# The lead-in of a transformer layer: small loads on another queue, the first conditioning columns computed another way

## The chip, the cores and the metric

The kernel runs on one core of a Trainium2 chip. Five engines take part, each with an instruction queue of its own that is worked off in order: TensorE (PE; its weight loads are listed as PEld), VectorE (DVE), ScalarE (ACT), GpSimd (POOL) and SyncE (SP), which here issues the DMA transfers. SBUF is the on-chip memory of 128 partitions; PSUM holds the sums of TensorE in banks of 128 x 512 FP32 numbers. The metric is the time of one execution in microseconds.

## The reference

One layer of a diffusion transformer in FP32: 256 latent tokens and 256 context tokens of width 2048. Cut to what matters here:

```
m = silu(cond) @ w_ada + b_ada             # cond: c for latent, c_ctx for context; w_ada: 2048 x 12288
sh1, sc1, g1, sh2, sc2, g2 = split(m, 6)
h = (x * (1 + sc1) + sh1) @ w_in           # latent;  w_in: 2048 x 3072
h_ctx = (ctx * (1 + csc1) + csh1) @ w_in   # context, with its own columns of m
... two kinds of attention over h and h_ctx, w_out, layer norm, SwiGLU FFN, layer norm
```

Before the first product with `w_in` can start, the conditioning vectors c and c_ctx must have gone through silu and through the columns of `w_ada` that belong to the first 128 features (a shift and a scale for each of the two token kinds), the first 128 columns of x and ctx must have been transposed and modulated, and the first rows of `w_in` must be there.

## The kernel before

Every large product is made of three products in a rounded FP32 form: a factor is split into a high part (a cast by ScalarE) and a low part (the remainder, by DVE), and TensorE adds high x high, high x low and low x high (`mm3`, L271 to L273). One such trio for a 128-token row block and 512 output columns takes three 128x512 products.

The first stage, the input projection, goes over the 16 blocks of 128 features in five groups of 1, 1, 2, 4 and 8 blocks (`GROUPS`). For group g the kernel needs:

- its conditioning columns (`flow_columns`): for shift and for scale the 2048 rows of `w_ada`, 128 columns per block. The weights are the moving operand, the columns of silu(c) the stationary one (`cs`, 32 columns wide); four partial sums land in four strips of a PSUM bank (L546). ScalarE copies them to SBUF (L571), TensorE adds the strips through a selection matrix (L576), and DVE adds the bias columns (L582, L584). The bias columns come from `brow`, a load of `b_ada` that TensorE transposes (L334).
- its part of x and ctx (`flow_part`, L608 and L613), transposed on TensorE (L633), modulated by ScalarE from PSUM into `uf` (L639), cast to the high part `uh` (L646), and subtracted by DVE to the low part `ul` (L649).
- its rows of `w_in` (`flow_weights`, loads at L473, high parts L495, low parts L498), in six blocks of 512 columns. Blocks 2 and 5 are keys and values and have four row blocks (two latent, two context); the others are queries and have two.

`flow_products` issues the trios, and `evac` (L696 to L700) takes the sums out of PSUM.

The order of all this is not the order in which it is written. `Flow` is a planner: each step is added with its engine, an assumed length, the steps that it follows and the buffers that it takes and gives back. `run` lays the steps out in time, engine by engine: whenever an engine is free, the ready step of lowest rank whose buffers are free goes next. Ranks are then recomputed from the latest start of each step, and the best of eight rounds is emitted. On the chip each engine works in that order, with real waits. The planner begins each engine at a given time (`F`'s second argument). Weights are loaded into six buffers of 1 MB (`raw`, four, and `araw`, two); 18 buffers of 512 KB (`b4`) hold modulated inputs, keys, values and other things.

56 warm-up steps (`warm_step`, L1130; two records each) are products of the identity that nobody reads. They depend on nothing but each other and have the lowest rank, so that the planner puts one wherever it sees TensorE free and no other step ready. They hold one of four PSUM work banks from the first to the last of them.

Ahead of the flow, in program order, stand the loads of c, c_ctx and `b_ada` (L311 to L314), the transpose of c and c_ctx (L316), its silu on ScalarE (L319) and the transpose of `b_ada`.

Of the kernel before, what the change touches and what calls it, by code (L numbers as in the profile page):

```python
# [196 lines left out]
def dit_layer(ctx: ExitStack, tc: tile.TileContext, x, c, cx, c_ctx, w_ada, b_ada, w_in, q_norm_g,  # L197
# [112 lines left out]
    crow = pa.tile([2 * KD, P], F32, tag="crow", name="crow")  # L310
    nc.sync.dma_start(crow[0:KD, :], c.rearrange("o (k p) -> (o k) p", p=P))  # L311
# [156 lines left out]
    def flow_load(w, k0, nk, c0, width, where=("raw", "araw")):  # L468
        room = Buf(*where)

        def fn():
            room.t = pools[room.pool].tile([P, G4 * NB], F32, tag="raw", name="raw")[:, : nk * width]
            nc.sync.dma_start(  # L473
                room.t.rearrange("p (k n) -> p k n", k=nk),
                w[k0 * P : (k0 + nk) * P, c0 : c0 + width].rearrange("(k p) n -> p k n", p=P),
            )

        return room, F.add("SP", dma_ns(nk * width * P * 4, width * 4), fn, take=[room])

    def flow_weights(w, k0, nk, c0, width=NB, where=("raw", "araw"), spare=False):  # L480

        raw, ld = flow_load(w, k0, nk, c0, width, where)
        pieces = []
        for s in range(0, nk * width, SUB * NB):
# [28 lines left out]

    def flow_products(hl, deps, ready, cols, ps, xs, first, last, prev):
# [16 lines left out]
    last_load = []  # L531

    def flow_columns(c0, ncol, shift, scale, ats, at):
# [18 lines left out]
        for g in range(ns):  # L552
# [3 lines left out]
            ns1 = nk / 4 * (40 + 1.67 * width)  # L556
            if c0:
                def both(g=g, r0=r0, r1=r1):
                    fn(g, 0, r0, 0, nk)
                    fn(g, 1, r1, 0, nk)  # L560

                prev = F.add("PE", 2 * ns1 + 420, both, [l0, l1, prev], [bank] if g == 0 else [], [r0, r1])
            else:
                prev = F.add("PE", ns1, lambda g=g, r=r0: fn(g, 0, r, 0, nk), [l0, prev], [bank] if g == 0 else [], [r0])
                prev = F.add("PE", ns1, lambda g=g, r=r1: fn(g, 1, r, 0, nk), [l1, prev], [], [r1])
        F.at = at
# [11 lines left out]
        def add(i):  # L578
# [4 lines left out]
            else:  # L583
                nc.vector.scalar_tensor_tensor(scale, pv[:, :, 1, :], 1.0, bc, op0=ALU.add, op1=ALU.add)  # L584

        a = F.add("ACT", 60 + 0.9 * width, copy, [prev], [sb], [bank])
        b = F.add("PE", 224 * ncol, sums, [a], [ps], [sb])
        return a, [F.add("DVE", 160, lambda i=i: add(i), [b], give=[ps]) for i in range(2)]

    u = {}  # L590

    def flow_inputs(g, span):
# [8 lines left out]
    def flow_part(k0, n, at, each):  # L601
# [13 lines left out]

        F.at = at + 0.5 * each if k0 else -2.0
        ns = dma_ns(n * P * SEQ * 4, n * P * 4)
        loads = [F.add("SP", max(ns, 500), load_x), F.add("SP", max(ns, 500), load_cx, take=[cx_room])]
        for s in range(2):
# [3 lines left out]
            for j0 in range(0, n, 2):  # L623
# [24 lines left out]
                def rest(rooms=rooms, j0=j0, nj=nj, uf=uf):  # L648
                    nc.vector.tensor_tensor(rooms[1].t[:, j0 : j0 + nj, :], uf.t[:, :nj, :],  # L649
                                            rooms[0].t[:, j0 : j0 + nj, :].bitcast(F32), op=ALU.subtract)  # L650

                p = F.add("PE", 205 * nj, flip, [loads[s], copy if k0 else None], [ps], [cx_room] if s else [],
                          at=None if k0 else -1.0)
                for j in range(nj):
# [7 lines left out]
    def flow_block(g, b, chunks):  # L662
# [10 lines left out]
        for (hl, deps), cols in chunks:  # L673
            kk = k0 + done
            base = kk - (kk - k0) % G4
            for r in rows:
# [3 lines left out]
                def operand(j, rooms=rooms, r=r):  # L680
# [463 lines left out]

    flow_inputs(0, (0.0, 0.0))
    T = 18.0
# [478 lines left out]
```

## Time and profile before

| | us |
|---|---|
| median of 3 runs | 1141.15 |
| lowest and highest run | 1140.55, 1144.86 |
| profiled execution: its span, which is its own time here | 1139.7 |
| first weight load issued by SyncE | 3.09 |
| first product with `w_in` | 18.58 |

The page of the profile has busy times per engine, the span in slices, the DMA queues, the chain of work that ended last, the costliest groups of instructions and the DMA issues. The views used below are: busy time by stretches (for each engine the busy microseconds and, in brackets, the number of instructions; then the granted clock of TensorE, the mean busy share of the 16 DMA engines and the GB/s that they moved); the timeline of an engine (start, duration, engine, line, operation, output<-inputs, shapes, count; in brackets the idle time before it and what ended it); groups of instructions by line (count, busy time, mean ns, idle time before them); waits (who waited for whom, in total, how often, the longest); and the chain of waits (start, duration, what). A busy TensorE is not necessarily doing needed work: the warm-up products count as busy.

### The profile page before, as it was taken

How to read it: one execution, taken by the hardware profiler on the slowest of the kernel's cores; microseconds unless marked ns; L12 is line 12 of the kernel's file. 1: busy time of each engine (PE TensorE's matmuls, PEld its weight loads, DVE VectorE, ACT ScalarE, POOL GpSimd, SP SyncE). 2: the span in 40 equal slices, each digit the busy share in tenths (PEclk: the TensorE clock that was granted, in tenths of full speed). 3: DMA queues.
4: the chain of work that ended last, by engine and by line, in shares of the span. 5: the costliest groups of instructions: out<-in, count | busy, mean ns of one | idle time of the engine just before them, and what ended most of it. 6: DMA issues, size and time to landing. Idle time of an engine off the chain costs nothing.

```text
span 1139.7 us, 14229 instructions
## 1 busy us (share of the span) xinstructions
PE 1119.6 (98%) x5347; PEld 905.9 (79%) x5347; DVE 828.2 (73%) x1053; ACT 546.7 (48%) x784; POOL 42.2 (4%) x82
## 2 busy tenths in 40 slices
PE   8999999999999999999999999999999999999995
PEld 8766678788887787888888888888888888888884
DVE  4753589899989896867767566776766787676556
ACT  3332454877874365444464444445444344333441
POOL 1000040110100000010000000000000000000000
PEclk9999999999999999999999999999999999999998
DMA  8999999776999688988866776677677888877531
GB/s 257 392 381 384 396 379 356 259 250 200 369 350 386 230 325 323 317 314 307 310 203 237 235 240 222 219 256 258 205 263 241 311 314 332 319 270 266 190 135 74
DMA packets 178078, 321.28 MB, mean 282 GB/s; under 512 B 8620, under 2 KB 42828, under 8 KB 175703
## 3 DMA queue, kind: packets, MB, share of 16 engines
q1 hardware_dynamic: 178008, 320.36, 80.2%
q8 instruction: 42, 0.69, 0.2%
q14 instruction: 28, 0.23, 0.1%
HBM read 304.07 MB, written 16.25 MB: 281 GB/s over the span
## 4 chain that ended last, share of the span: by engine, by line
PE 90%; DMA 5%; DVE 3%; ACT 1%; issue 0%; POOL 0%; SPq 0%; DVEq 0%; POOLq 0%; ACTq 0%
PE acc L271 27%; PE acc L273 27%; PE acc L272 27%; DMA raw<-in_w_ada_dram 2%; PE wk L546 2%; PE wk L939 2%; PE wk L1130 1%; DMA raw<-in_w_in_dram 1%; DMA raw<-in_w_out_dram 1%; DMA pd<-hx 1%; PE wk L271 1%; PE wk L273 1%; PE wk L272 1%; PE wk L633 1%; PE wk L992 0%; DVE lo L498 0%
## 5 line engine op out<-in xcount | busy, mean ns | idle before, releaser
L262 DVE TENSOR_TENSOR lo<-raw,hi 128x1024 fp32r<-128x1024 f32 x258 | 312.0, 1221 | 181.8 <-ACT hi L261 178.5
L261 ACT CAST hi<-raw 128x1024 fp32r<-128x1024 f32 x258 | 270.7, 1055 | 334.3 <-PE acc L273 296.3
L272 PE MATMUL acc<-lo,u2h 128*128 128x512 f32 x704 | 274.0, 389 | 0.8 <-DVE lo L262 0.8
L271 PE MATMUL acc<-hi,u2h 128*128 128x512 f32 x704 | 274.7, 390 | 0.0
L273 PE MATMUL acc<-hi,u2l 128*128 128x512 f32 x704 | 274.1, 389 | 0.1
L271 PEld LDWEIGHTS acc<-hi,u2h 128*128 128x128 f32 x704 | 132.2, 188 | 28.3 <-ACT u2h L1448 0.8
L272 PEld LDWEIGHTS acc<-lo,u2h 128*128 128x128 f32 x704 | 132.2, 188 | 28.2 <-DVE lo L262 1.1
L273 PEld LDWEIGHTS acc<-hi,u2l 128*128 128x128 f32 x704 | 132.2, 188 | 28.1 <-DVE u2l L1449 0.6
L495 ACT CAST hi<-raw 128x1024 fp32r<-128x1024 f32 (+1 forms) x86 | 87.8, 1031 | 116.8 <-DMA raw<-in_w_in_dram 63.8
L271 PE MATMUL acc<-hi,hTh 128*128 128x512 f32 x344 | 135.5, 394 | 0.0
L273 PE MATMUL acc<-hi,hTl 128*128 128x512 f32 x344 | 133.9, 389 | 0.0
L272 PE MATMUL acc<-lo,hTh 128*128 128x512 f32 x344 | 133.9, 389 | 0.0
L381 DVE SCALAR_TENSOR_TENSOR adav<-raw,cs,adav 128x512 f32<-128x512 f32 (+1 forms) x128 | 121.3, 948 | 13.4 <-DMA raw<-in_w_ada_dram 11.2
L498 DVE TENSOR_TENSOR lo<-raw,hi 128x1024 fp32r<-128x1024 f32 (+1 forms) x86 | 101.6, 1194 | 29.1 <-ACT hi L495 28.8
L271 PE MATMUL acc<-hi,uh 128*128 128x512 f32 x256 | 102.5, 400 | 0.2 <-ACT hi L495 0.2
L272 PE MATMUL acc<-lo,uh 128*128 128x512 f32 x256 | 100.2, 391 | 1.7 <-DVE lo L498 1.5
L273 PE MATMUL acc<-hi,ul 128*128 128x512 f32 x256 | 100.0, 390 | 0.0
L272 PEld LDWEIGHTS acc<-lo,hTh 128*128 128x128 f32 x344 | 64.6, 188 | 14.4 <-issue 1.0
L271 PEld LDWEIGHTS acc<-hi,hTh 128*128 128x128 f32 x344 | 64.6, 188 | 14.2 <-issue 0.7
L273 PEld LDWEIGHTS acc<-hi,hTl 128*128 128x128 f32 x344 | 64.6, 188 | 13.3
L271 PEld LDWEIGHTS acc<-hi,uh 128*128 128x128 f32 x256 | 48.1, 188 | 16.5 <-issue 5.9
L272 PEld LDWEIGHTS acc<-lo,uh 128*128 128x128 f32 x256 | 48.1, 188 | 11.8 <-DVE lo L498 2.6
(205 smaller groups left out, 1149.2 us busy)
## 6 DMA issues: line engine op xcount, KB each, us to landing
raw<-in_w_ada_dram SPq DMA_DIRECT2D x72, 1024.0 KB, 7.7
raw<-in_w_gate_dram SPq DMA_DIRECT2D x44, 1024.0 KB, 5.2
raw<-in_w_up_dram SPq DMA_DIRECT2D x44, 1024.0 KB, 5.3
raw<-in_w_down_dram SPq DMA_DIRECT2D x44, 1024.0 KB, 4.9
raw<-in_w_ada_dram SPq DMA_DIRECT2D x48, 512.0 KB, 5.5
raw<-in_w_in_dram SPq DMA_DIRECT2D x18, 1024.0 KB, 7.4
raw<-in_w_out_dram SPq DMA_DIRECT2D x16, 1024.0 KB, 8.0
pd<-hx SPq DMA_DIRECT2D x64, 128.0 KB, 3.8
```

The lines of the kernel that those rows point to most:

```text
L261: nc.scalar.copy(hi[:, :n], raw[:, s : s + n])
L262: nc.vector.tensor_tensor(lo[:, :n], raw[:, s : s + n], hi[:, :n].bitcast(F32), op=ALU.subtract)
L271: nc.tensor.matmul(ps, lhsT=xh, rhs=w[0], start=first, stop=False, skip_group_check=seeded)
L272: nc.tensor.matmul(ps, lhsT=xh, rhs=w[1], start=False, stop=False, skip_group_check=seeded)
L273: nc.tensor.matmul(ps, lhsT=xl, rhs=w[0], start=False, stop=last, skip_group_check=seeded)
L381: nc.vector.scalar_tensor_tensor(a[:, c : c + piece], raw[:, f : f + piece], cs[:, 4 * (g * (G4 * NB // w) + j) + 2, None], a[:, c : c + p ...
L495: nc.scalar.copy(hl.hi[:, :n], raw.t[:, s : s + n])
L498: nc.vector.tensor_tensor(hl.lo[:, :n], raw.t[:, s : s + n], hl.hi[:, :n].bitcast(F32), op=ALU.subtract)
L546: nc.tensor.matmul(bank.t[32 * j : 32 * j + 32, :width], lhsT=cs[:, 4 * k + 2 - 2 * i : 4 * k + 34 - 2 * i], rhs=raw.t[:, c * width : (c + ...
L633: nc.tensor.transpose(ps.t[:, (j * 2 + t) * P : (j * 2 + t + 1) * P], src, ident)
L939: nc.tensor.matmul(o_ps.t[:, : 2 * P].rearrange("p (g q) -> p g q", q=32), lhsT=v, rhs=pv[:, k], start=k == 0, stop=k == 3)
L1130: nc.tensor.matmul(wps, lhsT=ident, rhs=ident, start=True, stop=True)
```

## The change

Four things are changed at the start of the kernel, and the planner lays out the whole first flow anew with them.

1. The loads of c, c_ctx, the first 128 columns of x and ctx, and `b_ada` are issued from ScalarE's queue, in this order, ahead of its other instructions. The planner takes SyncE as free from 0.7 us, not 2.1. The tile for ctx's first columns is taken outside the planner.
2. Group 0's conditioning columns are computed by `first_columns`: each of the two 1 MB loads becomes four of 256 KB, the weights are the stationary operand and the two columns of silu(c), silu(c_ctx) the moving one. The sums come out with features on partitions, so the ScalarE copy and the sums through the selection matrix go, and DVE adds the bias to the PSUM result.
3. For groups of one block (groups 0 and 1) ScalarE writes the high part straight from PSUM while DVE computes the whole modulated value from PSUM and subtracts the high part from it. Before, ScalarE did the modulation and then the cast.
4. Group 0's rows of `w_in` are loaded into `b4` buffers and not into the 1 MB ones. Some order is fixed by hand: the casts of its later weights follow the high parts, the first low part follows the bias additions, and the four last row blocks of group 0 (block 5) each follow a step of group 1: its column sums, its small sums, its two transposes.

```diff
-    nc.sync.dma_start(crow[0:KD, :], c.rearrange("o (k p) -> (o k) p", p=P))
-    nc.sync.dma_start(crow[KD : 2 * KD, :], c_ctx.rearrange("(k p) -> k p", p=P))
+    nc.scalar.dma_start(crow[0:KD, :], c.rearrange("o (k p) -> (o k) p", p=P))
+    nc.scalar.dma_start(crow[KD : 2 * KD, :], c_ctx.rearrange("(k p) -> k p", p=P))
     brow = pa.tile([6 * KD, P], F32, tag="brow", name="brow")
-    nc.sync.dma_start(brow, b_ada.rearrange("o (n p) -> (o n) p", p=P))
+    cx0 = pa.tile([P, 2, NB], F32, tag="b4", name="cxt", bufs=NB4)
+    nc.scalar.dma_start(xt[:, :, :P], x[:, :P].rearrange("(t p) d -> p t d", p=P))
+    nc.scalar.dma_start(cx0[:, :, :P], cx[:, :P].rearrange("(t p) d -> p t d", p=P))
+    nc.scalar.dma_start(brow, b_ada.rearrange("o (n p) -> (o n) p", p=P))
...
-             {"SP": 2100.0, "PE": 3800.0, "ACT": 4300.0, "DVE": 4000.0, "POOL": 4000.0})
+             {"SP": 700.0, "PE": 3800.0, "ACT": 4300.0, "DVE": 4000.0, "POOL": 4000.0})
...
-    F.room["b4"] -= 4
+    F.room["b4"] -= 5
...
+            if room.pool == "b4":
+                room.t = b4([P, 2 * NB], F32, "raw1")[:, : nk * width]
...
-            a = F.add("ACT", 60 + 0.87 * n, cast, [ld], hl.rooms)
-            b = F.add("DVE", 60 + 1.06 * n, rest, [a], give=[raw])
+            a = F.add("ACT", 60 + 0.87 * n, cast, [ld, *after], hl.rooms)
+            b = F.add("DVE", 60 + 1.06 * n, rest, [a, *then], give=[raw])
...
-        after = [deps[0], (deps[1], 200), ready[0], (ready[1], 400), prev]
+        after = [deps[0], (deps[1], 200), ready[0], (ready[1], 400), prev, behind]
...
+    def first_columns(shift, scale, flips):
+        bank, prev, ready = Buf("wk"), None, []
+        for i in range(2):
+            raw, name = Buf("raw", "araw"), "raw"
+            def load(q, i=i, raw=raw):
+                if q == 0:
+                    raw.t = pools[raw.pool].tile([P, G4 * NB], F32, tag="raw", name="raw")
+                nc.sync.dma_start(
+                    raw.t[:, q * NB : (q + 1) * NB].rearrange("p (k n) -> p k n", k=4),
+                    w_ada[q * NB : (q + 1) * NB, i * D : i * D + P].rearrange("(k p) n -> p k n", p=P),
+                )
+            def sums(q, i=i, raw=raw):
+                if i == q == 0:
+                    bank.t = wk_bank()
+                for k in range(4 * q, 4 * q + 4):
+                    nc.tensor.matmul(bank.t[:, 4 * i : 4 * i + 2], lhsT=raw.t[:, k * P : (k + 1) * P],
+                                     rhs=cs[:, 4 * k + 2 : 4 * k + 4], start=k == 0, stop=k == KD - 1)
...
+            for q in range(4):
+                ld = F.add("SP", dma_ns(P * NB * 4, 512), lambda q=q, f=load: f(q), [], [raw] if q == 0 else [])
+                prev = F.add("PE", 900, lambda q=q, f=sums: f(q), [ld, prev, *(flips if i > q else ())], [bank] if i == q == 0 else [], [raw])
+            ready.append(F.add("DVE", 160, add, [prev], give=[bank]))
...
+    def first_inputs():
...
+        flips = [F.add("PE", 410, lambda s=s: flip(s), [], [banks[s]], [room] if s else []) for s in range(2)]
+        first_ready[:] = first_columns(shc[:, 0:1, :], scc[:, 0:1, :], flips)
...
+            def high(s=s, ps=ps, rooms=rooms):
+                rooms[0].t = b4([P, 4, SEQ], F32R, "uh")
+                rooms[1].t = b4([P, 4, SEQ], F32R, "ul")
+                nc.scalar.activation(rooms[0].t[:, 0, :], ps.t[:, :SEQ], AF.Identity,
+                                     bias=shc[:, 0, s : s + 1], scale=scc[:, 0, s : s + 1])
+            def whole(s=s, ps=ps, uf=uf):
+                uf.t = t2k("uf", (P, 2, SEQ))
+                nc.vector.tensor_scalar(uf.t[:, 0, :], ps.t[:, :SEQ], scc[:, 0, s : s + 1], shc[:, 0, s : s + 1],
+                                        op0=ALU.mult, op1=ALU.add)
...
-                                        done + len(cols) == ng, ends.get(r))
+                                        done + len(cols) == ng, ends.get(r),
+                                        column_steps[P][r] if (g, b) == (0, 5) else None)
...
-                piece, = flow_weights(w_in, k0, 1, b0 * NB, m * NB, where)
+                piece, = flow_weights(w_in, k0, 1, b0 * NB, m * NB, where if g else ("b4",),
+                                      after=() if g or not i else [u[0, s][1][0][0] for s in range(2)],
+                                      then=() if g or i else first_ready)
...
-    flow_inputs(0, (0.0, 0.0))
+    F.at = 0.0
+    first_inputs()
```

More of the change, by code (lines that the diff above doesn't have):

```diff
@@ L471, in fn @@
         def fn():
-            room.t = pools[room.pool].tile([P, G4 * NB], F32, tag="raw", name="raw")[:, : nk * width]
+            if room.pool == "b4":
+                room.t = b4([P, 2 * NB], F32, "raw1")[:, : nk * width]
+            else:
+                room.t = pools[room.pool].tile([P, G4 * NB], F32, tag="raw", name="raw")[:, : nk * width]
             nc.sync.dma_start(
@@ L478, in flow_load, with flow_weights @@
         return room, F.add("SP", dma_ns(nk * width * P * 4, width * 4), fn, take=[room])
-    def flow_weights(w, k0, nk, c0, width=NB, where=("raw", "araw"), spare=False):
+    def flow_weights(w, k0, nk, c0, width=NB, where=("raw", "araw"), spare=False, after=(), then=()):
         raw, ld = flow_load(w, k0, nk, c0, width, where)
@@ L512, in flow_seed, with flow_products @@
         return F.add("ACT", 475, fn, after, [ps])
-    def flow_products(hl, deps, ready, cols, ps, xs, first, last, prev):
+    def flow_products(hl, deps, ready, cols, ps, xs, first, last, prev, behind=None):
         seed = first and prev is not None
@@ new lines, in dit_layer, with flip, rest @@
+    u = {}
+    first_ready = []
+    def first_inputs():
+        room = Buf("b4")
+        room.pool = "b4"
+        banks = [Buf("wk") for _ in range(2)]
+        def flip(s):
+            banks[s].t = wk_bank()
+            for t in range(2):
+                nc.tensor.transpose(banks[s].t[:, t * P : (t + 1) * P], (cx0 if s else xt)[:, t, :P], ident)
+        flips = [F.add("PE", 410, lambda s=s: flip(s), [], [banks[s]], [room] if s else []) for s in range(2)]
+        first_ready[:] = first_columns(shc[:, 0:1, :], scc[:, 0:1, :], flips)
+        for s in range(2):
+            rooms, ps, uf = [Buf("b4"), Buf("b4")], banks[s], Buf("t2k")
+            u[0, s] = rooms, []
+            def high(s=s, ps=ps, rooms=rooms):
[7 more added lines that the diff above has]
+                                        op0=ALU.mult, op1=ALU.add)
+            def rest(uf=uf, rooms=rooms):
+                nc.vector.tensor_tensor(rooms[1].t[:, 0, :], uf.t[:, 0, :], rooms[0].t[:, 0, :].bitcast(F32), op=ALU.subtract)
+            a = F.add("ACT", 460, high, [flips[s], *first_ready], rooms, [ps])
+            b = F.add("DVE", 420, whole, [flips[s], *first_ready, *(b for _, b in u[0, 0][1])], [uf], [ps])
+            b = F.add("DVE", 350, rest, [a, b], give=[uf])
+            u[0, s][1].append((a, b))
@@ L650, in rest, with high, whole @@
                                             rooms[0].t[:, j0 : j0 + nj, :].bitcast(F32), op=ALU.subtract)
-                p = F.add("PE", 205 * nj, flip, [loads[s], copy if k0 else None], [ps], [cx_room] if s else [],
-                          at=None if k0 else -1.0)
+                def high(rooms=rooms, s=s, ps=ps):
+                    rooms[0].t = b4([P, 4, SEQ], F32R, "uh")
+                    rooms[1].t = b4([P, 4, SEQ], F32R, "ul")
+                    nc.scalar.activation(rooms[0].t[:, 0, :], ps.t[:, :SEQ], AF.Identity,
+                                         bias=shc[:, k0, s : s + 1], scale=scc[:, k0, s : s + 1])
+                def whole(s=s, ps=ps, uf=uf):
+                    uf.t = t2k("uf", (P, 2, SEQ))
+                    nc.vector.tensor_scalar(uf.t[:, 0, :], ps.t[:, :SEQ], scc[:, k0, s : s + 1], shc[:, k0, s : s + 1],
+                                            op0=ALU.mult, op1=ALU.add)
+                p = F.add("PE", 205 * nj, flip, [loads[s], copy], [ps], [cx_room] if s else [])
+                column_steps[k0 * P].append(p)
+                if n == 1:
+                    a = F.add("ACT", 460, high, [p] + ready, rooms, [ps])
+                    b = F.add("DVE", 420, whole, [p] + ready, [uf], [ps])
+                    b = F.add("DVE", 60 + 330 * nj, rest, [a, b], give=[uf])
+                    u[k0, s][1].append((a, b))
+                    continue
                 for j in range(nj):
```

26 lines of the change are left out of this document (16 added, 10 removed).

## The prediction

> **What bounds the kernel now.** I read the page's head first, then busy time by stretches, then TensorE's and SyncE's timelines of the first 37 us, the chain of waits there, and SyncE's own waits.
>
> ```profile
> span 1139.7 us, 14229 instructions
> PE 1119.6 (98%) x5347; PEld 905.9 (79%) x5347; DVE 828.2 (73%) x1053; ACT 546.7 (48%) x784; POOL 42.2 (4%) x82
> ```
>
> TensorE is busy for 98% of the span, so time is won only where it is busy with nothing useful. The stretches (columns: busy time of PE, PEld, DVE, ACT, POOL with instruction counts, granted clock, DMA share, GB/s) show the other resource:
>
> ```profile
> 0.00:5.00 5.00, 1.82 (x8) 1.72 (x9) 2.82 (x3) 1.75 (x3) 3.48 (x9) 1.00 0.32 89
> 5.00:13.00 8.00, 8.00 (x87) 7.68 (x86) 0.00 (x0) 0.00 (x0) 0.00 (x0) 1.00 1.04 321
> 13.00:16.50 3.50, 3.50 (x55) 3.18 (x54) 0.89 (x3) 1.77 (x3) 0.00 (x0) 1.00 0.35 79
> 16.50:20.00 3.50, 3.50 (x27) 3.28 (x27) 2.01 (x4) 2.68 (x7) 0.00 (x0) 1.00 0.97 321
> 20.00:24.00 4.00, 4.00 (x19) 3.27 (x19) 3.92 (x6) 1.54 (x4) 0.00 (x0) 1.00 1.18 312
> 24.00:30.00 6.00, 6.00 (x38) 4.75 (x40) 4.38 (x8) 2.87 (x5) 0.00 (x0) 1.00 1.11 372
> 30.00:80.00 50.00, 49.86 (x371) 34.92 (x363) 31.94 (x49) 15.91 (x24) 0.00 (x0) 1.00 1.04 385
> 80.00:150.00 70.00, 68.30 (x388) 46.62 (x387) 34.90 (x48) 28.79 (x46) 0.00 (x0) 1.00 1.03 394
> 150.00:320.00 170.00, 170.00 (x786) 139.03 (x784) 158.82 (x262) 117.37 (x247) 27.10 (x54) 1.00 0.85 296
> ```
>
> From 16.5 to 150 us both TensorE and the DMA engines are full (share about 1); from 150 to 320 TensorE alone. The DMA engines are under-used only at the start (share 0.32) and in 13 to 16.5 us (0.35). So a lead won in the first 30 us reaches the end only if the loads keep up until 150 us. TensorE's start:
>
> ```profile
> 14.20 1.08 PE L546 MATMUL wk<-raw,cs 128*32 128x128 f32 x32
> 15.21 0.94 PE L1130 MATMUL wk<-ident 128*128 128x128 f32 x6
> 15.98 0.28 PE L576 MATMUL wk<-sel,ada 128*128 128x4 f32 x2
> 16.12 2.70 PE L1130 MATMUL wk<-ident 128*128 128x128 f32 x22
> 18.58 0.48 PE L271 MATMUL acc<-hi,uh 128*128 128x512 f32 x1
> ...
> 29.68 1.96 PE L546 MATMUL wk<-raw,cs 128*32 128x128 f32 x64
> ```
>
> L1130 is filler: warm-up products that nobody reads. The first real product starts at 18.58 us, 3.3 us after the last column sums (14.20 + 1.08) end. In between run a ScalarE copy, the small sums of L576, two additions, two modulations, two casts and two subtractions, under 22 filler records. Group 0's products fill 18.58 to 29.68: 11.1 us. The wait for group 1's inputs, in the chain of waits:
>
> ```profile
> 31.64 0.86 PE wk L1130 x6
> 32.50 0.12 PE wk L576 x2
> 32.62 0.49 PE wk L633 x4
> 33.12 1.34 PE wk L1130 x12
> ```
>
> That is 0.86 + 1.34 = 2.2 us of filler after the first product, and it is all the filler but one step until 84 us.
>
> **The change part by part.**
>
> *Small loads on ScalarE's queue.*
>
> ```profile
> 0.73 0.40 SPq L311 DMA_DIRECT2D crow<-in_c_dram  x1
> 2.58 0.47 SPq L613 DMA_DIRECT2D cxt<-in_ctx_dram  x1
> 3.09 2.13 SPq L473 DMA_DIRECT2D raw<-in_w_ada_dram  x2
> 15.86 3.77 SPq L473 DMA_DIRECT2D raw<-in_w_ada_dram  x2
> ```
>
> Five issues leave SyncE, whose first weight load moves from 3.09 to 0.73 us: 2.36 us. On ScalarE they cost the same 2.3 us. The table load and the first activation queue behind them:
>
> ```profile
> 1.04 1.28 ACT L319 ACT_TABLE_LOAD   x1 [1.04 <-DVE cs L318]
> 3.35 0.23 ACT L319 ACTIVATE cs<-wk 128x32 f32<-128x32 f32 x1 [1.02 <-PE wk L316]
> ```
>
> They now run from about 3.05: cs is ready at 3.05 + 1.28 + 0.23 = 4.6 instead of 3.6 us. That is hidden as long as the bias rows (brow), now fifth, come no earlier: TensorE's transpose of them stands in its queue ahead of everything else.
>
> ```profile
> 1.65 1.77 DMA brow<-in_b_ada_dram
> 3.46 0.42 PE wk L334
> 5.64 0.43 PE wk L633 x2
> ```
>
> Issued at 2.6 and landing 1.77 later, brow is there at 4.4; but bulk loads now run beside it. I take 4.8, so TensorE is free for the flow at 5.2 (at least 4.8; at most 7.3, if brow needs the 4.3 us that the one weight load of the first 20 us with a landing of its own took, 2.6 + 4.3 + 0.42):
>
> ```profile
> DMA to landing us min/median/max: 4.3/4.3/4.3
> ```
>
> *First columns as stationary weights, in quarters.* Two 1 MB loads become eight of 256 KB. What precedes the last product is 2.1 MB of columns and 0.3 MB of small loads; at the row's 321 GB/s that takes 7.5 us from about 2.5 us on, so the last quarter is there near 10 to 10.6 us. The 32 products (64 records, since L546's 16 products above are x32) now load 128 columns and stream 2. The trace has this shape elsewhere:
>
> ```profile
> 384.30 1.84 PE L992 MATMUL wk<-ones,adav 128*128 128x2 f32 x16
> ```
>
> 1.84 / 16 = 0.115 us a record; 64 take 7.4 us, against 2 x 1.08 before, and the two transposes of x and ctx (2 x 0.43) stand among them. From 5.2 us TensorE ends these at 5.2 + 7.4 + 0.9 = 13.5: later than the loads, so TensorE and not the DMA sets this end. Bounds for a record, both from L576: 0.12 / 2 = 0.06 in the chain, 0.28 / 2 = 0.14 in the timeline, so 9.9 to 15 us with 5.2 kept.
>
> A rule of the Trainium skill speaks against the quarters: "DMA: Bandwidth & Descriptors", section Bandwidth, wants loads of 1 MiB or more, and its fit of 2 us plus bytes would make eight loads that follow one another about 21 us (an estimate from that page). The trace shows loads overlapping: 321 GB/s with several in flight. By the rows the term stays 13.5. By the rule the first product would come after 23 us (below, as a rival).
>
> *High parts from PSUM.* The ScalarE copy, the L576 sums and a cast go. What is left behind the last sums is DVE's, in its groups of 13 to 18.7 us:
>
> ```profile
> L649 DVE TENSOR_TENSOR ul<-uf,uh 128x256 fp32r<-128x256 f32 x2 | 0.8, 421 | 0.1
> L498 DVE TENSOR_TENSOR lo<-raw,hi 128x512 fp32r<-128x512 f32 x1 | 0.7, 693 | 10.2 <-ACT hi L495 10.2
> L584 DVE SCALAR_TENSOR_TENSOR scc<-wk,bcol 128x2 f32<-128x2 f32 x1 | 0.1, 149 | 0.0
> ```
>
> One addition 0.15, the first weight's low part 0.69 (it now waits for that addition), the modulated whole 0.42 (not in the trace; nearest is the 128x256 subtraction), the subtraction 0.42: 1.7 us. The third product of the first block needs it; so the first block runs as if it began at 13.5 + 1.7 - 0.4 = 14.8. **First term: 18.6 - 14.8 = -3.8 us** (at best the last quarter's landing plus its own sums and the chain, 10.3 + 0.5 + 1.3 = 12.1; at worst 7.3 + 64 x 0.14 + 0.9 + 1.3 = 18.5: -6.5 to -0.1). The same new form for group 1 adds two wholes on DVE (0.8 us) and takes two casts from ScalarE; both lie beside 11.1 us of products.
>
> *First weights in small buffers.* SyncE's fourth weight load waited; the gap of 13 to 16.5 us, 0.65 x 3.5 = 2.3 us of idle DMA, is that wait. With its own buffers that gap goes too. DMA lead: 2.36 to 2.36 + 2.3 = 4.7 us; I take 3.5, since extra space can only be filled as fast as SyncE issues.
>
> *Block 5 of group 0 behind group 1's columns.* The column sums, small sums and transposes of group 1 go between the last four rows of block 5, so the copy, addition and modulation run beside products. The 2.2 us of filler go if group 1's columns are there after twelve of the sixteen row blocks. Sixteen take 11.1 us, so at 14.8 + 8.3 = 23.1. Bytes: before, the rows sum to 5.66 MB by 24 us; 6.4 MB, at which group 1's columns are complete (2.4 as above, 1.6 of group 0's weights, 2.4 of group 1's columns and inputs), by 25.9. With 3.5 us of lead: 22.4. Just in time. **Second term: -2.0** (0 to -2.2).
>
> *Loads against the lead.* TensorE is then 5.8 us ahead, its loads only 3.5 (2.4 to 4.7), and they are saturated until 150 us. SyncE's queue shows both sides:
>
> ```profile
> SPq L473 <- PE wk L546: 36.4, 15, 6.9
> SPq L473 <- DVE lo L498: 14.5, 8, 4.2
> ```
>
> It waits 36 us for buffers that TensorE frees: an earlier TensorE lets loads be issued earlier, but not move faster. **Third term: +1.2** (0 to 5.8 - 2.4 = 3.4), nearer to the lower end because SyncE's waits for TensorE are that long, while TensorE's waits for weights, quoted next, are 1.5 us.
>
> *The warm-up steps.* There are 56 as before (112 records); the planner sets one wherever it sees TensorE with nothing ready.
>
> ```profile
> L1130 PE MATMUL wk<-ident x112: 274/275/474, 3.7 to 84.0; 128*128 128x128 f32 x112
> ```
>
> Less the 18 records of the chain above and the last step at 84 us, 92 records or 46 steps lay ahead of the first product. Now the sums fill that time: in the planner's list TensorE has eight sums and two transposes ahead of the first product, and a gap only in the 1.7 us of the chain behind them, room for some 8 steps. So 48 must go behind, where ten went before. Each costs 2.70 / 11 = 0.245 us if TensorE would not have waited anyway. Lower bound 0 (all in real waits, as the 2.2 us were), upper (48 - 10) x 0.245 = 9.3. TensorE's waits elsewhere, as its own rows give them, are few:
>
> ```profile
> PE acc L272 <- DVE lo L498: 1.5, 2, 0.8
> PE acc L273 <- DVE oTl L951: 1.0, 2, 0.9
> ```
>
> Most must find waits that the earlier products make (group 0's DVE work, group 2's inputs). **Fourth term: +1.7** (seven uncovered).
>
> Sum: -3.8 - 2.0 + 1.2 + 1.7 = -2.9: a span of 1136.8. The profiled execution's 1139.7 lies 1.45 under the median of 1141.15, so the median goes to **1138.2 us**. A measurement of this kernel tells 0.5% (5.7 us) from no change.
>
> **The rivals.** *The whole lead arrives.* Third and fourth terms near 0 and the first somewhat larger: -5.8 to -8, 1133.2 to 1135.3 us. For it: TensorE's waits are few, and SyncE waits for it rather than the reverse. Against: DMA share 1.03 to 1.04 until 150 us.
>
> *Warm-up steps on the path (slower).* The 38 additional steps run between real products or at the flow's end. The kernel is slower than before from 2.9 / 0.245 = 12 more uncovered steps on, 19 in all; with all 38 it is -2.9 - 1.7 + 9.3 = +4.7: 1145.9. For it: 170 of 170 us busy after 150 us; no room to hide. Against: the planner sets them only in gaps of its own reckoning.
>
> *The lead is hidden.* The loads of 30 to 150 us set the pace and arrive as before, because the buffers fill as before: 1141 us. For it: 385 and 394 GB/s, the same in both long stretches. Against: those waits for buffers.
>
> *Quarters one after another.* Each pays a landing of 1.77 and 0.8 for its data: 8 x 2.6 = 21 us, first product near 24, +5.4 - 2.0: 1144.6. This is what the Trainium skill's rule (same page and section) would do here. The trace disagrees, with two loads issued 0.5 us apart sharing 321 GB/s.
>
> **How the numbers follow.** Forecast 0.49 (own range 1135.5 to 1141), whole lead 0.22, warm-up steps 0.17, hidden 0.09, quarters in turn 0.03. Below 1135.4 lies the second case: faster 0.22. Above 1146.9 lie only the warm-up and quarters cases together with later loads: slower 0.05. Within 0.5%: 0.73. The range 1133.5 to 1143.5 leaves out the far ends of the whole-lead and warm-up cases, about 0.17.
>
> **What would show it.** Right: first L473 issue near 0.7 us; the new column sums in 64 records of about 0.115; first product at 14 to 15.5 us; no DMA share of 0.35 in 13 to 16.5; the column sums of group 1 (x64) among group 0's products and no filler of 2.2 us behind them; more waits for weights between 40 and 130 us. Wrong: warm-up records in numbers after 150 us, or a first product before 13 us with no new waits, would move the time up or down as the rivals say.

## The result, and the profile after

The changed kernel takes 1168.89 us (median; 1165.11 to 1170.12), the kernel before beside it 1141.06: a ratio of 1.0227, 95% interval 1.0204 to 1.025. It is slower by 27.8 us; the prediction was 1138.2 us. The span of the profiled execution is 1166.9 us, 27.2 more than that of before. (A span is a little shorter than the time of the same execution, which here is 1168.72 us.)

The head of the page after:

```profile
span 1166.9 us, 14226 instructions
PE 1136.6 (97%) x5345; PEld 919.9 (79%) x5345; DVE 830.9 (71%) x1057; ACT 546.4 (47%) x779; POOL 40.0 (3%) x82
```

TensorE runs two instructions fewer than before and is busy for 17 us longer; the other 10 us it stands idle, 4 of them at the start (4.41 + 2.62 + 0.33 us in the rows below, against 3.03 + 0.15 before). TensorE's timeline of the lead-in after (columns as in the prediction):

```profile
4.41 0.28 PE L319 MATMUL wk<-ident,crow 32*128 32x32 f32 x1 [4.41 <-DMA crow<-in_c_ctx_dram]
7.31 0.42 PE L337 MATMUL wk<-ident,brow 96*128 96x96 f32 x1 [2.62 <-DMA brow<-in_b_ada_dram]
...
8.38 8.53 PE L613 MATMUL wk<-cs,raw 128*128 128x2 f32 x40
17.24 5.28 PE L613 MATMUL wk<-cs,raw 128*128 128x2 f32 x24 [0.33 <-DVE shc L619]
22.38 3.33 PE L1229 MATMUL wk<-ident 128*128 128x128 f32 x14
25.37 0.77 PE L271 MATMUL acc<-hi,uh 128*128 128x512 f32 x1
25.94 0.63 PE L272 MATMUL acc<-lo,uh 128*128 128x512 f32 x1
26.36 0.63 PE L273 MATMUL acc<-hi,ul 128*128 128x512 f32 x1
...
27.85 0.40 PE L271 MATMUL acc<-hi,uh 128*128 128x512 f32 x1
28.08 0.39 PE L272 MATMUL acc<-lo,uh 128*128 128x512 f32 x1
```

The first product comes at 25.37, not at 18.58 as before. The 64 two-column products (L613) take 8.38 to 22.38, 0.22 us each. The products begin 0.42 us apart at 26 and 0.23 us apart at 28: TensorE has half its speed until about 27.5 us. Before, the fillers ran at full speed from about 7 us on, so the first product found the full clock.

Where the rest is lost shows in the start of TensorE's products by their input: `uh` (input projection), `oTh` (w_out), `u2h` (first half of the FFN). Each row has the count, the shortest, median and longest duration in ns, and the first and last start in us. Before:

```profile
L271 PE MATMUL acc<-hi,uh x256: 389/389/582, 18.6 to 256.8; 128*128 128x512 f32 x128
L271 PE MATMUL acc<-hi,oTh x128: 389/389/792, 257.5 to 389.5; 128*128 128x512 f32 x128
L271 PE MATMUL acc<-hi,u2h x704: 389/389/501, 394.3 to 882.8; 128*128 128x512 f32 x176
```

After:

```profile
L271 PE MATMUL acc<-hi,uh x256: 389/389/774, 25.4 to 276.3; 128*128 128x512 f32 x128
L271 PE MATMUL acc<-hi,oTh x128: 387/389/796, 277.0 to 410.9; 128*128 128x512 f32 x128
L271 PE MATMUL acc<-hi,u2h x704: 387/389/774, 416.0 to 910.2; 128*128 128x512 f32 x176
```

The delay is 6.8 us at the first product, 19.5 at the end of the input projection (277.0 - 257.5), 21.7 at the first `u2h` and 27.4 at the last. Most of the loss thus lies behind the lead-in that was changed. What stands there is filler. The group of the warm-up products after, and two rows of the timeline:

```profile
L1229 PE MATMUL wk<-ident x112: 270/275/561, 22.4 to 253.2; 128*128 128x128 f32 x112
```

```profile
32.87 1.50 PE L1229 MATMUL wk<-ident 128*128 128x128 f32 x12
...
137.02 1.73 PE L1229 MATMUL wk<-ident 128*128 128x128 f32 x14
```

Before, 92 of the 112 records ran ahead of the first product; now 14 do, and 98 (49 steps) run among real work up to 253 us. By the last row a record occupies TensorE for 0.111 us ((1.73 - 0.28) / 13), so these 98 take 10.9 us. TensorE's waits between 30 and 480 us after (who waited for whom: total us, times, longest):

```profile
PE wk L1400 <- DVE xt L1164: 2.0, 1, 2.0
PE wk L578 <- ACT ada L573: 1.7, 1, 1.7
PE acc L271 <- ACT acc L516: 1.5, 1, 1.5
PE acc L271 <- ACT oTh L1045: 1.2, 1, 1.2
PE acc L272 <- DVE lo L504: 1.0, 2, 0.7
PE wk L1038 <- ACT pr L1000: 0.7, 1, 0.7
```

They sum to 8.1 us. Before, the same view has 3.5 us (1.5 + 1.0 + 0.8 + 0.2). A further wait of 1.7 us, for a low part of weights at 614 us, lies behind this window and has no counterpart before. The longest of all is followed by a loss of clock, in the stretches after (columns as in the prediction; the last three are clock, DMA share, GB/s):

```profile
410.00:420.00 10.00, 10.00 (x62) 5.68 (x60) 7.87 (x24) 2.81 (x7) 0.53 (x1) 1.00 0.52 178
420.00:423.50 3.50, 1.47 (x9) 1.06 (x8) 2.78 (x8) 0.67 (x2) 0.00 (x0) 1.00 1.02 362
423.50:430.30 6.80, 6.80 (x21) 5.62 (x21) 3.65 (x10) 3.10 (x7) 0.95 (x1) 0.50 0.27 104
```

6.8 us at a clock of 0.50 lose 3.4 us. (In the first 27 us this column reads 1.00, which the products' spacing of 0.42 us contradicts; the durations decide there.)

### The profile page after: what moved, and what is told of

It is laid out like the page before. It is cut to its first block, busy times and chain, and to the rows that moved or that the text cites. A ratio compares the mean times of both kernels' runs of the same rounds, so it can differ in the third digit from the quotient of the medians.

```text
span 1166.9 us, 14226 instructions
## 1 busy us (share of the span) xinstructions
PE 1136.6 (97%) x5345; PEld 919.9 (79%) x5345; DVE 830.9 (71%) x1057; ACT 546.4 (47%) x779; POOL 40.0 (3%) x82
## 4 chain that ended last, share of the span: by engine, by line
PE 88%; DVE 5%; DMA 4%; ACT 1%; issue 1%; SPq 0%; ACTq 0%; DVEq 0%
PE acc L271 26%; PE acc L272 26%; PE acc L273 26%; PE wk L552 2%; PE wk L1038 1%; DMA raw<-in_w_in_dram 1%; DMA raw<-in_w_ada_dram 1%; PE wk L1229 1%; PE wk L613 1%; DVE lo L504 1%; DVE adav L384 1%; PE wk L712 1%; DMA pd<-hx 1%; DMA lgb<-in_ln_b_dram 1%; DVE m L988 0%
## 5 line engine op out<-in xcount | busy, mean ns | idle before, releaser
L273 PEld LDWEIGHTS acc<-hi,hTl 128*128 128x128 f32 x344 | 64.6, 188 | 13.3
L273 PEld LDWEIGHTS acc<-hi,ul 128*128 128x128 f32 x256 | 48.4, 189 | 10.5 <-DVE ul L728 0.2
```

Source lines behind the costliest of these rows:

```text
L273: nc.tensor.matmul(ps, lhsT=xl, rhs=w[0], start=False, stop=last, skip_group_check=seeded)
```

## The experiments

The theory: the loss is the warm-up steps that no longer fit ahead of the first product, now among real products. The rivals: the late first product itself (+6.8 us, handed on and enlarged by loads and buffers), the warm-up steps' PSUM bank, and the small loads. "The changed kernel" below is the kernel after.

**Fewer warm-up steps.** The changed kernel with 7 steps (shown), and with 34:

```diff
-WARM = 56
+WARM = 7
```

> The changed kernel with 7 warm-up steps instead of 56, so that all of them (14 records) lie ahead of the first product; nothing else is edited. The theory of the warm-up steps on the path: the 98 records behind the first product, 0.111 us each, cost their 10.9 us, so the median falls from 1168.9 to about 1158, and the 22 steps of 248 to 253 us go with nothing in their place. The rival, that they only fill waits: no more than 2 us less, and TensorE waits in their places. The clock theory (TensorE runs at half clock while it does two-column products) expects the lead-in unchanged: first product near 25.4 us, full clock from about 27.5 us.

> The changed kernel with 34 warm-up steps: the 22 steps that ran from 248 to 253 us go, and the bank comes free at about 150 us. If the steps cost only their own time, 22 x 0.222 = 4.9 us less than the changed kernel, 1164 us. If they cost through the bank and through what comes later in the order too, 1152 to 1159 us.

With 7 steps: 1146.21 us, ratio to the kernel before 1.0044 (1.0027 to 1.006). With 34: 1156.12 us, 1.0121 (1.01 to 1.0141). So 49 steps cost 22.7 us of the 27.8, twice what was expected of them. The first 27 cost 9.9 us (6.0 by their own time), the other 22 cost 12.8 (4.9). Product starts with 7 steps:

```profile
L271 PE MATMUL acc<-hi,uh x256: 387/389/711, 25.4 to 260.9; 128*128 128x512 f32 x128
L271 PE MATMUL acc<-hi,oTh x128: 389/389/792, 261.5 to 392.6; 128*128 128x512 f32 x128
L271 PE MATMUL acc<-hi,u2h x704: 387/389/501, 397.3 to 886.3; 128*128 128x512 f32 x176
```

The first product is as late as in the changed kernel (25.4), and all that remains of it at the last `u2h` is 3.5 us (886.3 - 882.8). The rival "late first product, enlarged" falls: it explains about 5 us by the medians (1146.21 against 1141.56 beside it), no more.

**The same steps without the change.** The kernel before with 49 steps more:

```diff
-WARM = 56
+WARM = 105
```

> The kernel before with 105 warm-up steps and not 56: 49 steps more, as many as the changed kernel shed when it fell from 56 to 7, with nothing else of the change. If the price of steps that don't fit ahead of the first product is independent of the change (their own time of 0.22 us each and what they do to the order and the PSUM work banks), this kernel is slower than before by 10.9 us at least (49 x 0.22) and up to 23 us: 1152 to 1164 us. The nearer to 1164, the more of the extra price belongs to the steps themselves and to the bank that they hold; at 1152 the extra 12 us of the changed kernel come from the steps together with the change's new order. If the planner hides them (rival: they fall in real waits), below 1147.

1153.41 us against 1140.54 beside it, ratio 1.0112 (1.0081 to 1.0144). In both kernels 92 records run ahead of the first product, so all 98 added ones run behind it:

```profile
L271 PE MATMUL acc<-hi,uh x256: 387/389/586, 18.4 to 264.1; 128*128 128x512 f32 x128
...
L271 PE MATMUL acc<-hi,u2h x704: 388/389/497, 406.8 to 894.2; 128*128 128x512 f32 x176
```

The last `u2h` is 11.4 us later than before, little more than the steps' own 10.9 (the median says 12.9, with some 4 us either way). Its waits in the same view sum to 3.3 us, as before. So a step that doesn't fit costs about its own time in the old order, and the 12 us beyond it in the changed kernel belong to the steps together with that kernel's order, not to the steps alone.

**The bank.** The planner of the changed kernel with 7 steps gets three work banks; and the changed kernel with all 56 steps, each of which takes and returns its own bank:

```diff
-    F = Flow({..., "wk": 4, ...
+    F = Flow({..., "wk": 3, ...
```

```diff
-    wps = Buf("wk")
...
     def warm_step(i):
-        if i == 0:
-            wps.t = wk_bank()[:, :P]
-        warm(wps.t, 1)
+        warm(wk_bank()[:, :P], 1)
...
     for i in range(WARM):
-        warms.append(F.add("PE", 225, ..., [warms[-1]], [wps] if i == 0 else [], [wps], at=1e6))
+        wps = Buf("wk")
+        warms.append(F.add("PE", 225, ..., [warms[-1]], [wps], [wps], at=1e6))
```

> The changed kernel with 7 warm-up steps, and with the planner given three PSUM work banks instead of four for the whole first flow. The warm-up steps hold one of the four from the first to the last of them, in the changed kernel until 253 us. Theory that this held bank makes up what the 49 later steps cost beyond their own 10.9 us (11.8 us): 5 to 12 us slower than the run with 7 steps and four banks, 1151 to 1158 us. Rival (the bank does not matter, the steps disturb the order or the waits in another way): within 2 us of 1146.2.

> The changed kernel with all 56 warm-up steps, each taking a PSUM bank of its own and giving it back, instead of one bank held from the first step to the last. Theory that the 49 later steps cost their own 10.9 us and the rest (11.8 us) through the held bank: 1146.2 + 10.9 = 1157, within 3 us. Rival (the rest comes from where the steps stand, not from the bank): 1164 us or more.

Three banks: 1153.94 us, 1.0102 (1.0082 to 1.0122), 7.7 us over the same kernel with four. Own banks: 1161.32 us, 1.0165 (1.0149 to 1.0181), 7.6 us under the changed kernel, between the two expectations. The two sizes agree, which alone doesn't show one cause. With three banks and hardly any filler the wait and the loss of clock are back. Waits, then stretches, of that kernel:

```profile
PE wk L1400 <- DVE xt L1164: 2.0, 1, 2.0
```

```profile
411.00:418.00 7.00, 7.00 (x23) 5.82 (x22) 2.95 (x9) 2.93 (x8) 0.95 (x1) 0.52 0.51 169
```

Neither stands in the kernels with 7 steps, with 34, with own banks, or with 105 steps in the old order. Wait and clock are 2.0 + 3.4 = 5.4 of the 7.6 us. But the changed kernel gives the bank back with the last step at 253 us, and the wait comes at 420: TensorE doesn't wait for that bank. In the old order with 105 steps the bank is held until the last step at 402 us, and no such wait follows. So what the bank changes is most likely the order that the planner settles on. Why that order comes in the new code and not in the old one is not settled, and whether any other small change of what the planner is given would move the order as far was not tried.

**The clock in the lead-in.** The changed kernel with 7 steps and 14 identity products (28 records) right behind the transpose of c:

```diff
+    hps = wk_bank()[:, :P]
+    for _ in range(14):
+        nc.tensor.matmul(hps, lhsT=ident, rhs=ident, start=True, stop=True)
```

> As the run with 7 warm-up steps, with 14 products of the identity (28 records) put right behind the transpose of c, where TensorE waited from 4.7 to 7.3 us for the bias rows. Clock theory: full clock from about 8 to 10 us, the column sums at 0.115 us a record instead of 0.21, so 7.4 us instead of 14.1, and the first product near 18 to 19 us: about 7 us less than the run beside it. Rival (the two-column product with 128 columns to load is slow by its shape at either clock): 0.21 us a record as before, first product at 26 us or later, time as the run beside it or longer. Between the two: the clock is granted and taken away again while the sums run; then part of the records take 0.115 and the later ones 0.21, and the gain is 2 to 5 us.

1144.69 us, 1.0033 (1.0022 to 1.0044). Timeline:

```profile
4.70 4.96 PE L338 MATMUL wk<-ident 128*128 128x128 f32 x28
...
10.02 4.53 PE L616 MATMUL wk<-cs,raw 128*128 128x2 f32 x40
14.87 5.28 PE L616 MATMUL wk<-cs,raw 128*128 128x2 f32 x24 [0.33 <-DVE shc L622]
20.02 3.33 PE L1232 MATMUL wk<-ident 128*128 128x128 f32 x14
23.00 0.77 PE L271 MATMUL acc<-hi,uh 128*128 128x512 f32 x1
```

and stretches:

```profile
8.00:15.00 7.00, 6.67 (x61) 6.59 (x59) 0.16 (x1) 0.86 (x2) 0.00 (x0) 0.99 1.09 380
15.00:25.00 10.00, 10.00 (x43) 9.61 (x44) 4.61 (x8) 3.75 (x6) 0.00 (x0) 0.50 1.07 333
```

After the identity products the first 40 sums run at 0.11 us a record (4.53 / 40), the price of the prediction. Then the clock falls to 0.50 and the other 24 take 0.22 each, though TensorE was idle for 0.33 us only. So both prices belong to the clock, and the two-column products neither bring the full clock nor keep it. This is the third of the cases above. The first product comes 2.4 us earlier than with 7 steps alone; the median is 1.5 us lower, but the two intervals overlap.

**The old form of the columns.** The changed kernel with weights as moving operand, with 56 steps and with 37 (as many as lie ahead of its first product, and two more):

```diff
-        first_ready[:] = first_columns(shc[:, 0:1, :], scc[:, 0:1, :], flips)
+        first_ready[:] = flow_columns(0, 1, shc[:, 0:1, :], scc[:, 0:1, :], [0.0], 0.0)[1]
```

> The changed kernel with group 0's conditioning columns computed as before (two 1 MB loads, weights as the moving operand, copy and selection sums), all other parts of the change kept, 56 warm-up steps. Clock theory: the planner has 24 warm-up steps ahead of the column sums again, full clock from 9 to 12 us, first product near 17 us, so 8 us earlier than in the changed kernel; with the rest of the change as it is, 1158 to 1161 us. Rival (the loss lies in the loads or in the later order, not in how the columns are computed): within 3 us of 1168.9.

> The kernel with moving column weights and the rest of the change, with 37 warm-up steps instead of 56, so that none is left after 32 us. Theory of the steps on the path: the 19 steps (38 records, 4.2 us) go, 1140 to 1142.5 us, no slower than the kernel before. Rival (they only filled waits there): 1145 to 1147 us.

56 steps: 1146.51 us, 1.0051 (1.0033 to 1.0068). 37 steps: 1144.42 us, 1.002 (1.0006 to 1.0033). The first product comes at 20.6 and 21.1 us. With 56 steps the time lies under both expectations, with 37 between them. 35 steps are ahead of the first product again, 21 behind it, and the 19 that the second run leaves out cost 2.1 us, half of their own time (4.2): in this order some of them do fall in waits. So the form of the columns, with its loads, decides where the steps land, and that decides the 22 us. Against the stationary form with 7 steps (1146.21) the old form with 37 is 1.8 us faster by the medians; the intervals overlap.

**The small loads.** Part 1 of the change alone on the kernel before (with 40 steps, to keep them ahead of the first product); and the old form with 37 steps with the load of `b_ada` third in ScalarE's queue, not fifth. The diff shows the first of the five loads (those of x and ctx leave the planner):

```diff
-    nc.sync.dma_start(crow[0:KD, :], ...)
+    nc.scalar.dma_start(crow[0:KD, :], ...)
...
-             {"SP": 2100.0, ...
+             {"SP": 700.0, ...
```

> Part 1 alone on the kernel before: the five small loads on ScalarE's queue, SyncE's first weight load at 0.7 us, 40 warm-up steps (35 lie ahead of the first product). Theory that the small loads land late because bulk loads now run beside them (c at 6 instead of 3 us, bias rows at 7 to 9 instead of 3.4): TensorE starts 3 us later, the first product at 18 to 20 us, 1141 to 1144 us. Rival (an earlier weight stream is a gain of its own): first product near 16.5 us, 1138 to 1140 us.

> As the run beside it with moving column weights and 37 steps, with the bias rows third in ScalarE's queue, ahead of x and ctx. Theory that TensorE's start hangs on the bias rows (their transpose stands ahead of everything, and they landed at 7.3 us): TensorE's flow starts 1 to 2 us earlier and the first product comes 1 to 2 us earlier; 1 to 2 us less than the run beside it. Rival (their late landing is due to the bulk loads, not to their place): the transpose still starts after 6.5 us, and the time is the same.

Part 1 alone: 1142.94 us, 1.0018 (1.0006 to 1.0029): it makes the kernel slower by about 2 us (0.7 to 3.3), as its theory said, though the first product is later than that theory's 20 us. Its timeline:

```profile
6.26 0.28 PE L319 MATMUL wk<-ident,crow 32*128 32x32 f32 x1 [6.26 <-DMA crow<-in_c_ctx_dram]
9.05 0.42 PE L337 MATMUL wk<-ident,brow 96*128 96x96 f32 x1 [2.51 <-DMA brow<-in_b_ada_dram]
...
21.58 0.48 PE L271 MATMUL acc<-hi,uh 128*128 128x512 f32 x1
```

On SyncE's queue ahead of the weights, `b_ada` was there for its transpose at 3.46 us; beside them it comes at 9.05, c at 6.26, and the first product at 21.58 instead of 18.58. With `b_ada` third: 1144.05 us, 1.0011 (0.9998 to 1.0024). Its transpose comes at 7.26 instead of 8.96, but x and ctx are then late, and the first product comes at 22.3, not at 21.1; the time is the same, as the rival said. Whichever is last beside the weight loads sets the start. ScalarE's queue alone doesn't make the loads late: in the same place on it c_ctx landed 3.0 us after its issue in the changed kernel, beside loads of 256 KB, and 4.9 us after it here, beside loads of 1 MB. The Trainium skill ("DMA: Bandwidth & Descriptors", section "Issuing engines are not separate DMA queues") says that transfers share the same engines whoever issues them, and that issuing from a second engine saves only issue time. The trace agrees and adds a price: 2.36 us of issue saved, 3.2 us (c) and 5.6 us (`b_ada`) of arrival lost.

**What the warm-up is worth.** The kernel before without warm-up steps:

```diff
-WARM = 56
+WARM = 0
```

> The kernel before without its 56 warm-up steps. Clock theory: TensorE is at half clock until 3.5 to 5 us of its own work have passed, so the column sums and the first 8 to 12 products of 512 columns take twice as long; the first product can start earlier than 18.58 us, since no filler stands ahead of it, and the time is 1 to 5 us longer than before. Rival (the filler is only filler): 1 to 3 us shorter than before.

1142.0 us, 1.0002 (0.999 to 1.0013). The first product comes at 17.44, 1.1 us earlier, and the half clock lasts until 23 us. The time is that of the kernel before, which neither expectation had. One offsets the other: the steps that cost 22.7 us in the changed kernel gain nothing that can be measured in the kernel before.

**The parts that might win.** Small loads c, c_ctx and `b_ada` on SyncE ahead of the weights, x and ctx on ScalarE's queue, the old form of the columns with its two halves as steps of their own, and parts 3 and 4 as in the change; 37 steps, and SyncE taken as free from 2.1 us again. Of the three loads the first is shown, and the change of the column form, shown above, is left out:

```diff
-    nc.scalar.dma_start(crow[0:KD, :], ...)
+    nc.sync.dma_start(crow[0:KD, :], ...)
...
-            prev = F.add("PE", 2 * ns1 + 420, both, [l0, l1, prev], ...)
+            if c0:
+                prev = F.add("PE", 2 * ns1 + 420, both, [l0, l1, prev], ...)
+            else:
+                prev = F.add("PE", ns1, ..., [l0, prev], ...)
+                prev = F.add("PE", ns1, ..., [l1, prev], [], [r1])
```

> A version made of the parts that the runs do not speak against: c, c_ctx and the bias rows first on SyncE's queue as before, x and ctx on ScalarE's, columns with moving weights in two steps as before, high parts from PSUM, first weights in small buffers, block 5 behind group 1's columns, 37 warm-up steps, all of them ahead of the first product. Theory that the loss lay in two-column sums, late small loads and leftover steps: first product at 16.5 to 17.5 us, 1138 to 1140.5 us, faster than the kernel before by 0.1 to 0.3%. Rival (what is gained at the first product is lost again by 90 us, because the loads are full from 20 us on and stop where buffers are not free): 1141 to 1143 us.

1140.77 us, 0.9992 (0.9983 to 1.0001): the same as before, between the two expectations. Group 1's small sums and the use of the DMA engines are what the prediction wanted; the first product comes 0.8 us earlier than before, not 3.8. Timeline and stretches:

```profile
17.80 0.48 PE L271 MATMUL acc<-hi,uh 128*128 128x512 f32 x1
...
29.64 0.28 PE L582 MATMUL wk<-sel,ada 128*128 128x4 f32 x2
```

```profile
13.00:16.50 3.50, 3.50 (x55) 3.18 (x54) 0.27 (x3) 0.89 (x2) 0.00 (x0) 1.00 1.08 367
...
30.00:80.00 50.00, 49.28 (x307) 33.11 (x307) 33.53 (x54) 15.82 (x23) 0.00 (x0) 1.00 1.01 372
80.00:150.00 70.00, 68.15 (x383) 46.60 (x382) 35.80 (x47) 29.05 (x47) 0.00 (x0) 1.00 1.04 394
```

No DMA gap is left at 13 to 16.5 us, and group 1's small sums stand among group 0's products. Group 1's first product starts at 32.4 us, 3.9 earlier than before, but the kernel before has by then done half of group 2's column sums as well, 1.9 us of work:

```profile
34.39 1.93 PE L546 MATMUL wk<-raw,cs 128*32 128x256 f32 x32
```

So the lead in work is 2.0 us. At 53 us, when both kernels have done the same sums, it is 0.9, at 84 us 1.0 and at 151 us 1.1. The DMA engines are full from 30 to 150 us here as before, and the loads take back about half of what the start wins: in the chain of waits the column sums at 51.18 us follow a load of `w_ada` that was issued at 40.72, behind the sums that freed its buffer, and took 9.90 us.

## Why the prediction was wrong

- **Fourth term, warm-up steps: +1.7, measured +22.7.** This is the step that failed: 21.0 of the 30.7 us between the forecast and the result. The count was right (48 steps behind the first product; 49 are), and so was the price of one (0.245 us; 0.22). Wrong was that most would "find waits that the earlier products make". In the changed kernel they find none: the waits grew from 3.5 to 8.1 us beside them. The old order with 49 steps more shows what a step in the way costs, its own time: 11.4 us. The upper bound of 9.3 took only the steps over the ten of before and only their own time; it left out that the planner, given 49 products more, finds another order. By rows of the changed kernel against the one with 7 steps (23.9 us between the profiled executions): 10.9 own time, 6.8 more of waits (8.1 + 1.7 - 3.0), 3.4 of lost clock; 2.8 are not assigned. Against the one with 34 steps (13.3 us) the same working gives 4.9 + 5.4 + 3.4 = 13.7, so what the last 22 steps cost beyond their own time is these waits and the clock. Why the order brings them stays open.
- **First term, first product: 14.8 forecast, 25.37 measured.** The sums were priced at 0.115 us a record from a row far inside the kernel, at full clock; they took 0.22. That is 6.6 of the 10.6 us, and above the upper bound (0.14), because the bounds came from rows at the full clock and the clock of the lead-in was never asked about. `b_ada` was taken at 4.8 and came at 7.31, so that TensorE was free for the flow at 7.53, just above the upper bound of 7.3; the sums start 2.3 us later than the forecast's 6.1. The other 1.7 lie between the last sum and the first product (3.0 us). (Between the last sums and the first product of the kernel before, the rows show 28 filler records, 6 and 22, not 22; no term rests on that.)
- **What the first term is worth.** With 7 steps a first product 6.8 us late makes the end 4.7 us late. About 2 us of that may go with the small loads (part 1 alone) and 1.8 with the form of the columns; this is an estimate from medians whose intervals overlap, and what is left is within the intervals.
- **Second term, group 1's wait: -2.0.** The mechanism is there, at about the size forecast. From the first product to group 1's first, the kernel before takes 17.7 us, or 15.8 without group 2's sums at 34.39 us; the combined version takes 14.6 (-1.2) and the changed kernel with 7 steps 14.1 (-1.7). In the changed kernel itself it is lost: the interval is 17.3 us, with 20 filler records (29.22 to 34.13 us) and the half clock in it.
- **Third term, loads against the lead: +1.2.** About right where there is a lead: the combined version hands back 0.9 to 1.1 of its 2.0 us. The changed kernel has none, and its loads have no lead either: its DMA share is 0.84 from 30 to 80 us, against 1.04 before:

```profile
20.00:24.00 4.00, 4.00 (x19) 4.00 (x20) 1.31 (x4) 0.61 (x2) 0.00 (x0) 1.00 0.47 140
...
30.00:80.00 50.00, 50.00 (x369) 36.74 (x371) 34.00 (x53) 14.46 (x22) 0.00 (x0) 1.00 0.84 293
```

- **The rivals.** "Warm-up steps on the path" was the right one, at 0.17, and its price of 1145.9 too low by its bound. "Quarters one after another" had nearly the right start (24 us) for a wrong reason: the sums waited 0.33 us in all, for an addition by DVE and not for a load, and the DMA engines moved 332 to 364 GB/s under them up to 20 us. (The fit that the prediction takes from the Trainium skill's page "DMA: Bandwidth & Descriptors" stands there in the section "Anatomy of one DMA", for transfers issued by GpSimd; these were issued by SyncE.) "The lead is hidden" comes near the combined version, which keeps about 1 us.
- **The sign "wrong if"** named warm-up records in numbers after 150 us; there are 46.

## What to carry to other kernels

Filler that is placed by a planner is work like any other once the gap that it was cut for closes: when a change fills an idle stretch, count the filler that stood there and cut it in the same change. Price an operation of the lead-in by the clock that the lead-in has, not by a row from the middle of the kernel. Small loads that start a chain belong ahead of the bulk loads in time; a second queue beside them doesn't protect them.

## What the runs showed of the hardware that was not expected

- Products of 128 stationary columns and two moving ones neither brought the full clock nor kept it. In the changed kernel 14.0 us of them at a stretch, with one pause of 0.33 us, leave TensorE at half speed; behind identity products the first 40 records ran at full clock, 4.5 us, and then it was lost (0.50 from 15 us). The Trainium skill ("TensorE: Matmul & The Clock Gate", Part 1, "What's actually happening") lets about 3.4 us of sustained busy time release the clock. For identity products the trace agrees: they start 0.21 us apart at first and 0.11 us apart from 8.0 us on, 3.3 us after they begin. For the two-column products it does not.
- One wait of 2.03 us was followed by 6.8 us at a clock of 0.50, so a single short wait in the middle cost 5.4 us. A wait of 2.00 us in the kernel with three banks was followed by the same. Waits of 1.70 us (the changed kernel, 614 us) and 1.94 us (`b_ada` third, 354 us) were not: the products behind them start 0.23 us apart.
- The load of `b_ada`, which landed 1.8 us after its issue when it went ahead of the weights, took 4.4 us beside them (issued at 2.93, transposed at 7.31), on another engine's queue.
